# Moving four sums of a weight pair and a sum of squares from GpSimd's arithmetic to transfers and VectorE, and one PSUM copy to ScalarE

## The chip, the cores and the metric

The kernel runs on one core of a Trainium2 chip. Its time is the device time of one execution in microseconds. Names of the engines as the profile writes them: PE is TensorE (PEld its weight loads), DVE is VectorE, ACT is ScalarE, POOL is GpSimd, SP is the engine that issues most transfers. SPq, ACTq and POOLq are the queues from which transfers are issued.

## The reference, cut to what matters

One step of two trunk layers of a streaming encoder over 656 tokens (528 prompt rows with 16 learned ones, 128 sample rows), all in float32. Each layer is a feed-forward part, a mixer (pooling, short convolution, attention, gates, `w_out`), and a second feed-forward part:

```python
def swiglu(x, w_gate, w_up, w_down):
    return (jax.nn.silu(x @ w_gate) * (x @ w_up)) @ w_down

h = x + 0.5 * swiglu(rmsnorm(x, n1), f1g, f1u, f1d)      # 1024 -> 2816 -> 1024
...                                                       # mixer, added to h
h = h + 0.5 * swiglu(rmsnorm(h, n2), f2g, f2u, f2d)
```

The change touches only how the gate and up products (`x @ w_gate`, `x @ w_up`) get their weights, how one of their blocks leaves PSUM, and how the mean of squares of an rmsnorm is summed.

## The kernel before, in words

Activations stand transposed: 128 features in the partitions, tokens along the row. A float32 product is made of three passes over a high and a low part of weight and activation (`mm3`), so each weight block is split by a copy on ACT and a subtraction on DVE into a "slab" (`prep_next`, L338; the tile is called `ws` or `slabs`, 128x2x4x128).

Gate and up columns are worked in **pairs** of two 128-column blocks (`pair_unit`, L615). The pair is a 2x2 block matrix a11, a12, a21, a22 (`A1` holds a11 and a12, `A2` holds a21 and a22; both are raw weights as loaded, 512 KB each) and it is multiplied in seven block products instead of eight, in the manner of Strassen and Winograd. Besides raw blocks this wants four sums of weights (`sums`, L391): s3 = a11 + a21 (into a buffer of its own in the tile `Wa`, two of them in turn), a21 += a22, a11 += a21, a12 += a11, the last three in place. The seven slabs are, in order, a11, a12, the summed a21, the summed a11, the summed a12, s3 and the raw a22 (`prep_pair`, L385). There are 80 pairs: ten gate and ten up pairs in each of four feed-forward parts.

`run_pair` (L687) runs the seven products of 12 matmuls each (`seven`) into three PSUM banks. Bank b1 (tile `mm`) takes four of them one after the other: B11, Q2, T3 and T4. Between two of them the bank's content is copied out: after B11 and Q2 by ACT, after T3 by DVE as s[3] = b1 + p5 (L719). T4 adds to the same bank, so its first matmul waits until the reader after T3 is done. T4 is held back (`late`) until the first product of the next pair has been issued. T4's own result leaves by `stt`.

Loads go through four raw buffers in turn; a pair takes two and a down unit one. A buffer's next load waits for the last reader of the old content. Slabs have eight places; a slab's place comes free when its matmuls are done. Units follow each other as gate pair, eight down units of the chunk before, up pair, then gate and up pairs in turn.

After each `w_down` or `w_out` product of the last chunk `feed` (L508) adds the square of the new rows to a running sum `acc`: eight squares by ACT, of which the first starts the sum, numbers two to seven are added by POOL (L528), and the eighth by DVE. Then matmuls with a matrix of ones (`scales`) give the row scales for the next part. This happens five times; there are 30 POOL additions in all.

The order of instructions within each engine is set by a scheduler that reorders independent instructions; every engine, and every queue that issues transfers, then runs its instructions strictly in that order and each waits for what it needs.

Of the kernel before, what the change touches and what calls it, by code (L numbers as in the profile page):

```python
# [7 lines left out]
AF = mybir.ActivationFunctionType  # L8
ALU = mybir.AluOpType

P = 128
# [45 lines left out]
class Builder:  # L57
# [261 lines left out]
    def load_next(self):  # L319
        u = self.units[self.n_load]  # L320
        if self.n_done < u["after"]:
            return False
        spots = self.take("raw", len(u["src"]), u["ring"] == "F")
        if spots is None:
            return False
        u["raw"] = []
        for at, (k, parts) in zip(spots, u["src"]):
            raw = at
            if raw is None:
                raw = self.rp.tile([P, KD * P], F32, tag="raw", name=self.name("raw"))  # L330
            raw = raw.rearrange("p (k c) -> p k c", k=KD)[:, :k, :]
            for k0, kn, src in parts:
                self.nc.sync.dma_start(raw[:, k0:k0 + kn, :], src.rearrange("(k p) c -> p k c", p=P))
            u["raw"].append((at, raw))
        self.n_load += 1
        return True

# [47 lines left out]
    def prep_pair(self, u, i):  # L385
# [2 lines left out]
        s3 = self.s3[u["turn"]].rearrange("p (k c) -> p k c", k=4)  # L388
        return (A1[:, 0:4], A1[:, 4:8], A2[:, 0:4], A1[:, 0:4], A1[:, 4:8], s3, A2[:, 4:8])[i]

    def sums(self, u, i):  # L391
        if i == 1:
            (_, A1), (_, A2) = u["raw"]
            add = lambda out, a, b: self.nc.gpsimd.tensor_tensor(out, a, b, op=ALU.add)  # L394
            s3 = self.s3[u["turn"]].rearrange("p (k c) -> p k c", k=4)
            a11, a12, a21, a22 = A1[:, 0:4], A1[:, 4:8], A2[:, 0:4], A2[:, 4:8]
            add(s3, a11, a21)
            add(a21, a21, a22)
            add(a11, a21, a11)
            add(a12, a11, a12)  # L400


    def run_units(self, units):
# [104 lines left out]
    def feed(self, to, l, m, hi):  # L508

        c0, c1 = self.halves[hi]  # L510
        gain = {"mixer": "mix_norm", "ffn1": "ffn1_norm", "ffn2": "ffn2_norm"}[to]
        if to == "mixer":
            self.gained(self.H[:, m, c0:c1], l, m, c0, c1, gain)
        if hi == 0:
            return
        c0 = self.halves[0][0]
        n = c1 - c0
        if to != "mixer":
            self.blocks(l, m, gain, c0, n // 2)
        acc, s = self.acc[:, :n], self.sq[self.fed % 2][:, :n]  # L520
        if self.fed == 0:
            self.act(acc, self.H[:, m, c0:c1], AF.Square)
        else:
            self.act(s, self.H[:, m, c0:c1], AF.Square)
            if self.fed == KD - 1:
                self.tt(acc, acc, s, ALU.add)
            else:
                self.nc.gpsimd.tensor_tensor(acc, acc, s, op=ALU.add)  # L528
        self.fed += 1
        if self.fed == KD:  # L530
            self.fed = 0
            halves = self.halves
            self.pending = lambda: self.scales(to, halves)
# [81 lines left out]
    def pair_unit(self, w, f, run, **kw):  # L615

        c = [slice((f + r) * P, (f + r + 1) * P) for r in range(2)]
        self.turn = not self.turn
        return dict(slabs=[4] * 7, src=[(KD, [(0, KD, w[:, x])]) for x in c], prep=self.prep_pair, then=self.sums,
                    run=self.run_pair, evict=run, ring="F", turn=int(self.turn), **kw)  # L620

    def col_unit(self, w, f, r, run):

# [63 lines left out]
    def run_pair(self, u):  # L687

        c0 = self.halves[0][0]
        n = self.halves[0][1] - c0  # L690
        b1, b2, b3 = self.psum("mm"), self.psum("z"), self.psum("z")
        p5 = self.copies[u["turn"]][:, :n]
        f = self.factor[:, c0:c0 + 2 * n]
        S = self.sil if u["evict"] == self.gate_out else self.up
        S = S[:, :4 * n]
        s = [S[:, i * n:(i + 1) * n] for i in range(4)]
        self.clock += 1
        self.seven(u, b1, B11, n, True)
        self.act(s[0], b1[:, :n], AF.Copy)
        self.pump(1)  # L700
        if self.late:
            self.late()
        self.finish_pending()
        self.seven(u, b3, B21, n, True)
        self.tt(s[0], b3[:, :n], s[0], ALU.add)
        self.pump(1)
        self.seven(u, b2, Q1, n, True)
        self.act(p5, b2[:, :n], AF.Copy)
        self.pump(1)
        self.seven(u, b1, Q2, n, False)  # L710
        self.act(s[1], b1[:, :n], AF.Copy)
        self.pump(1)
        self.seven(u, b2, B22, n, False)
        self.tt(s[1], b2[:, :n], s[1], ALU.add)
        self.mul(S[:, :2 * n], S[:, :2 * n], f)
        u["evict"](u, 0, n)
        self.pump(1)
        self.seven(u, b1, T3, n, False)
        self.tt(s[3], b1[:, :n], p5, ALU.add)  # L719
        self.stt(s[3], s[3], -1.0, f[:, n:], ALU.mult, ALU.mult)  # L720
        self.pump(1)

        def last():
            self.late = None
            self.seven(u, b1, T4, n, False)
            self.stt(s[2], b1[:, :n], -1.0, f[:, :n], ALU.mult, ALU.mult)
            u["evict"](u, 1, n)
            self.pump(1)
        self.late = last
        self.slot_tail()  # L730
# [507 lines left out]
    def token_scale(self, hi, sums):  # L1238
        c0, c1 = HALF_ALL[hi]
        self.scale_of(sums, c0, c1, False, self.sil, self.up)  # L1240
# [343 lines left out]
```

## Time and profile before

| what | value |
| --- | --- |
| time, median of 3 | 2890.72 us (2889.88 to 2891.71) |
| the profiled execution | 2890.04 us, its span 2888.3 us |
| PE busy | 2829.0 us, 98% of the span |
| DVE, ACT, POOL busy | 1936.6, 1289.9, 598.2 us |
| granted TensorE clock, mean | 0.994 |
| DMA | 224.27 MB, mean 78 GB/s, busy share of the 16 engines 26.2% for the SP queue |

Busy PE time is nearly the whole span, so what can be read for a change is in the 59 us in which PE is not busy: which wait, at which place, and what released it. The rest of the engines matter as far as they end those waits.

### The profile page before, as it was taken

Reading aid. Unit: us, or ns where it says so; the run is one execution under the profiler, and the core shown is the slowest. Engines: PE = TensorE matmul, PEld = TensorE weight load, DVE = VectorE, ACT = ScalarE, POOL = GpSimd, SP = SyncE. Lnnn points to the kernel's source line nnn. Section 1 sums busy time; section 2 is a strip of 40 time slices with the busy share of each in tenths; the row PEclk is TensorE's granted clock in tenths of the full one; section 3 lists DMA queues with packets and bytes.
Section 4 is the critical chain, followed back from the end, with each engine's and each line's share of the span. In section 5 each row is a group of like instructions: output and inputs, shape, how many; then the busy total and the mean of one; then the engine's idle time right before and its main releaser. Section 6 shows DMA issues by size and latency. Waiting matters only on the chain.

```text
span 2888.3 us, 47733 instructions
## 1 busy us (share of the span) xinstructions
PE 2829.0 (98%) x19179; PEld 2781.5 (96%) x19179; DVE 1936.6 (67%) x3262; ACT 1289.9 (45%) x2464; POOL 598.2 (21%) x481
## 2 busy tenths in 40 slices
PE   7999999999999999999999999999999999999999
PEld 6999999999999999999999999999999999999999
DVE  8686675876444877675786675768764458675764
ACT  5343344776323443343443443447763234343433
POOL 2233231011000123132223241311110002232230
PEclk8999999999999999999999999999999999999999
DMA  3222322222222322222312322222222223223222
GB/s 113 81 86 69 88 76 74 79 77 69 66 74 74 88 81 66 82 80 74 88 52 81 88 74 81 83 71 72 75 73 66 79 75 88 76 67 92 81 71 76
DMA packets 437169, 224.27 MB, mean 78 GB/s; under 512 B 10110, under 2 KB 436290, under 8 KB 436946
## 3 DMA queue, kind: packets, MB, share of 16 engines
q1 hardware_dynamic: 436452, 220.90, 26.2%
q8 instruction: 150, 2.46, 0.3%
q14 instruction: 73, 0.60, 0.1%
q10 hardware_dynamic: 494, 0.32, 0.0%
HBM read 212.87 MB, written 8.31 MB: 77 GB/s over the span
## 4 chain that ended last, share of the span: by engine, by line
PE 81%; DVE 10%; POOL 4%; DMA 3%; ACT 1%; issue 1%; ACTq 0%; SPq 0%; POOLq 0%; DVEq 0%
PE z L143 50%; PE mm L143 29%; DVE Wa L134 2%; DMA rawb<-in_ffn_w_up_dram 2%; DVE ws L134 2%; DVE Wa L131 2%; DVE slabs L134 2%; POOL rawb L394 1%; POOL raw L394 1%; DVE XR L134 1%; POOL Wa L394 1%; DMA raw<-in_ffn_w_gate_dram 1%; PE aux L143 1%; ACT ws L120 0%; DVE ra L134 0%
## 5 line engine op out<-in xcount | busy, mean ns | idle before, releaser
L143 PE MATMUL mm<-XR,ws 128*128 128x328 f32 (+3 forms) x4848 | 802.6, 314 | 12.6 <-DVE Wa L134 12.6
L143 PEld LDWEIGHTS mm<-XR,ws 128*128 128x128 f32 x4848 | 738.0, 188 | 20.4 <-DVE Wa L134 16.0
L143 PE MATMUL z<-XR,ws 128*128 128x328 f32 (+3 forms) x3924 | 629.2, 313 | 13.5 <-ACT XR L120 6.5
L143 PEld LDWEIGHTS z<-XR,ws 128*128 128x128 f32 x3924 | 597.1, 189 | 15.3 <-ACT XR L120 6.8
L134 DVE TENSOR_TENSOR ws<-raw,ws 128x512 fp32r<-128x512 f32 (+1 forms) x429 | 311.2, 728 | 175.8 <-ACT ws L120 174.0
L143 PE MATMUL z<-ra,ws 128*128 128x328 f32 (+1 forms) x2688 | 421.0, 312 | 0.2
L120 ACT ACTIVATE ws<-raw 128x512 fp32r<-128x512 f32 (+1 forms) x429 | 263.5, 617 | 338.2 <-PE z L143 192.7
L143 PEld LDWEIGHTS z<-ra,ws 128*128 128x128 f32 x2688 | 405.1, 188 | 0.7 <-ACT ra L120 0.4
L143 PE MATMUL z<-ra,slabs 128*128 128x328 f32 (+1 forms) x2112 | 330.9, 312 | 1.8 <-ACT ra L120 1.8
L143 PE MATMUL mm<-XR,slabs 128*128 128x328 f32 (+1 forms) x1944 | 318.9, 312 | 7.9 <-DVE Wa L134 7.7
L143 PEld LDWEIGHTS z<-ra,slabs 128*128 128x128 f32 x2112 | 319.3, 188 | 2.9 <-ACT ra L120 2.4
L143 PEld LDWEIGHTS mm<-XR,slabs 128*128 128x128 f32 x1944 | 296.4, 188 | 10.6 <-DVE Wa L134 9.8
L143 PE MATMUL z<-XR,slabs 128*128 128x328 f32 (+1 forms) x1764 | 296.6, 316 | 9.7 <-DVE Wa L134 6.5
L143 PEld LDWEIGHTS z<-XR,slabs 128*128 128x128 f32 x1764 | 275.1, 192 | 11.2 <-DVE Wa L134 7.0
L131 DVE SCALAR_TENSOR_TENSOR H<-z,H 128x328 f32<-128x328 f32 (+1 forms) x288 | 140.9, 492 | 130.5 <-PE z L143 130.1
L134 DVE TENSOR_TENSOR Wa<-Wa 128x656 f32<-128x656 f32 (+5 forms) x245 | 204.3, 834 | 3.9 <-ACT Wa L120 0.2
L134 DVE TENSOR_TENSOR ws<-rawb,ws 128x512 fp32r<-128x512 f32 (+1 forms) x183 | 147.9, 812 | 83.2 <-ACT ws L120 82.9
L120 ACT ACTIVATE slabs<-raw 128x512 fp32r<-128x512 f32 (+1 forms) x183 | 109.0, 600 | 209.9 <-PE z L143 86.1
L120 ACT ACTIVATE Wa<-Wa 128x656 f32<-128x656 f32 (+7 forms) x232 | 136.9, 597 | 122.6 <-DVE Wa L134 113.6
L134 DVE TENSOR_TENSOR slabs<-raw,slabs 128x512 fp32r<-128x512 f32 (+1 forms) x183 | 145.9, 799 | 61.7 <-ACT slabs L120 61.5
L120 ACT ACTIVATE ws<-rawb 128x512 fp32r<-128x512 f32 (+1 forms) x183 | 108.3, 599 | 172.5 <-PE z L143 94.7
L528 POOL TENSOR_TENSOR Wa<-Wa 128x656 f32<-128x656 f32 (+1 forms) x30 | 55.1, 1837 | 628.7 <-ACT Wa L120 602.5
(177 smaller groups left out, 2943.4 us busy)
## 6 DMA issues: line engine op xcount, KB each, us to landing
raw<-in_w_in_dram SPq DMA_DIRECT2D x88, 512.0 KB, 3.8
raw<-in_ffn_w_gate_dram SPq DMA_DIRECT2D x57, 512.0 KB, 3.7
rawb<-in_ffn_w_up_dram SPq DMA_DIRECT2D x55, 512.0 KB, 4.3
rawb<-in_ffn_w_down_dram SPq DMA_DIRECT2D x48, 384.0 KB, 3.4
raw<-in_ffn_w_down_dram SPq DMA_DIRECT2D x48, 384.0 KB, 3.4
raw<-in_ffn_w_up_dram SPq DMA_DIRECT2D x33, 512.0 KB, 3.7
rawb<-in_ffn_w_gate_dram SPq DMA_DIRECT2D x31, 512.0 KB, 3.8
raw<-in_w_out_dram SPq DMA_DIRECT2D x16, 512.0 KB, 3.9
```

The costliest lines, as they stand in the source:

```text
L120: i = self.nc.scalar.activation(out, in_, func, **kw).ins
L131: return self.nc.vector.scalar_tensor_tensor(out, in0, scalar, in1, op0=op0, op1=op1).ins
L134: self.nc.vector.tensor_tensor(out, in0, in1, op=op)
L143: self.nc.tensor.matmul(out, lhsT, rhs, start=start, stop=stop, skip_group_check=True)
L394: add = lambda out, a, b: self.nc.gpsimd.tensor_tensor(out, a, b, op=ALU.add)
L528: self.nc.gpsimd.tensor_tensor(acc, acc, s, op=ALU.add)
```

## The change

Two of the four sums are made by transfers that add to what stands at their destination (`grow`, issued from POOL's queue with `accum_op`), as soon as the weights are loaded: a21 += a22, and s3, into which a21 is first loaded from DRAM once more (256 KB on SP's queue) and to which a11 is then added. The other two, a11 += a21 and a12 += a11, become DVE additions, issued when slab 2 has been prepared. POOL's additions of squares become adding transfers too. The copy of bank b1 after T3 goes to ACT, and DVE adds p5 afterwards, from SBUF to SBUF.

```diff
@@ load_next, after the raw loads of a unit @@
+        if "turn" in u:
+            self.early_sums(u)
@@
+    def early_sums(self, u):
+        (_, A1), (_, A2) = u["raw"]
+        s3 = self.s3[u["turn"]].rearrange("p (k c) -> p k c", k=4)
+        self.nc.sync.dma_start(s3, u["a21"])
+        self.grow(A2[:, 0:4], A2[:, 4:8])
+        self.grow(s3, A1[:, 0:4])
+
     def sums(self, u, i):
-        if i == 1:
+        if i == 2:
             (_, A1), (_, A2) = u["raw"]
-            add = lambda out, a, b: self.nc.gpsimd.tensor_tensor(out, a, b, op=ALU.add)
-            s3 = self.s3[u["turn"]].rearrange("p (k c) -> p k c", k=4)
-            a11, a12, a21, a22 = A1[:, 0:4], A1[:, 4:8], A2[:, 0:4], A2[:, 4:8]
-            add(s3, a11, a21)
-            add(a21, a21, a22)
-            add(a11, a21, a11)
-            add(a12, a11, a12)
+            self.tt(A1[:, 0:4], A2[:, 0:4], A1[:, 0:4], ALU.add)
+            self.tt(A1[:, 4:8], A1[:, 0:4], A1[:, 4:8], ALU.add)
+
+    def grow(self, to, by):
+        self.nc.gpsimd.dma_start(to, by, accum_op=ALU.add)
@@ feed @@
-                self.nc.gpsimd.tensor_tensor(acc, acc, s, op=ALU.add)
+                self.grow(acc, s)
@@ run_pair, after T3 @@
-        self.tt(s[3], b1[:, :n], p5, ALU.add)
+        self.act(s[3], b1[:, :n], AF.Copy)
+        self.tt(s[3], s[3], p5, ALU.add)
```

The scheduler gives other orders. First POOL, at the last gate pair of the first feed-forward part (its weights are raw_249 and raw_250, those of the up pairs beside it rawb, s3 a part of Wa). Before:

```order
L394 TENSOR_TENSOR Wa_86<-raw_249_3611,raw_250_3613 128x512
L394 TENSOR_TENSOR raw_250_3613<-raw_250_3613 128x512
L394 TENSOR_TENSOR rawb_3_105<-rawb_3_105 128x512 x2
L394 TENSOR_TENSOR Wa_86<-rawb_3_105 128x512
L394 TENSOR_TENSOR rawb_3_105<-rawb_3_105 128x512
L394 TENSOR_TENSOR raw_249_3611<-raw_250_3613,raw_249_3611 128x512
L394 TENSOR_TENSOR raw_249_3611<-raw_249_3611 128x512
```

The same pair with the one before and the one after it, of the change:

```order
L410 DMA Wa_86<-rawb_3_105 128x512
L410 DMA rawb_3_105<-rawb_3_105 128x512
L410 DMA Wa_86<-raw_249_3647 128x512
L410 DMA raw_250_3649<-raw_250_3649 128x512
L410 DMA Wa_86<-rawb_3_105 128x512
L410 DMA rawb_3_105<-rawb_3_105 128x512
```

Before, the third and fourth sum of the gate pair stand behind the first two sums of the up pair that is loaded after it; now each pair has two transfers, and nothing of a pair stands behind the next pair's.

Then the reader of bank b1 after T3 (mm_255), which T4 waits for: before on DVE, in the same pair's neighbour.

```order
L134 TENSOR_TENSOR Wa_86<-z_256_3720,Wa_86 128x328
L134 TENSOR_TENSOR Wa_86<-Wa_86 128x656
L134 TENSOR_TENSOR ws_259_3803<-raw_249_3611,ws_259_3803 128x512
L134 TENSOR_TENSOR Wa_86<-Wa_86 128x656
L134 TENSOR_TENSOR ws_260_3823<-raw_249_3611,ws_260_3823 128x512
L134 TENSOR_TENSOR ws_261_3840<-Wa_86,ws_261_3840 128x512
L134 TENSOR_TENSOR Wa_86<-mm_255_3719,Wa_86 128x328
```

Of the change it is on ACT, where the copy of the summed a21 (ws_258) and those of the other sums (ws_259, ws_260, ws_261) stand in the same queue:

```order
L120 ACTIVATE ws_254_3737<-rawb_3_105 128x512
L120 ACTIVATE ws_258_3824<-raw_250_3649 128x512
L120 ACTIVATE slabs_2_104<-Wa_86 128x512
L120 ACTIVATE Wa_86<-mm_246_3631 128x328
...
L120 ACTIVATE ws_259_3842<-raw_249_3647 128x512
L120 ACTIVATE ws_260_3862<-raw_249_3647 128x512
L120 ACTIVATE ws_261_3880<-Wa_86 128x512
...
L120 ACTIVATE ra_41_550<-Wa_86 128x656
L120 ACTIVATE Wa_86<-mm_255_3757 128x328
```

The reader of the bank has moved from a place behind three DVE subtractions of slabs to one behind their three copies on ACT, and the copy of the summed a21 stands ahead of the previous pair's s3 slab.

## Rows read from the trace of the kernel before

**Rows 1.** The page's part 1: busy time, share of the span, instructions.

```profile
PE 2829.0 (98%) x19179; PEld 2781.5 (96%) x19179; DVE 1936.6 (67%) x3262; ACT 1289.9 (45%) x2464; POOL 598.2 (21%) x481
```

**Rows 2.** Waits of PE over the span: total us, times, longest.

```profile
PE mm L143 <- DVE Wa L134: 20.3, 19, 1.8
PE z L143 <- DVE Wa L134: 10.1, 3, 3.9
PE z L143 <- DVE XR L134: 5.8, 2, 3.3
```

**Rows 3.** Timeline of PE in the second mixer: start, length, idle before.

```profile
1940.00 5.33 PE L143 MATMUL mm<-XR,ws 128*128 128x384 f32 x20 [1.77 <-DVE Wa L134]
```

**Rows 4.** Timeline of all engines, 406 to 418 us.

```profile
406.40 1.30 POOL L394 TENSOR_TENSOR Wa<-rawb 128x512 f32<-128x512 f32 x1 [8.53 <-DMA rawb<-in_ffn_w_up_dram]
...
409.51 1.28 POOL L394 TENSOR_TENSOR raw<-raw,raw 128x512 f32<-128x512 f32 x1
...
410.83 0.63 ACT L120 ACTIVATE ws<-raw 128x512 fp32r<-128x512 f32 x1 [5.76 <-POOL raw L394]
...
411.49 1.22 DVE L134 TENSOR_TENSOR ws<-raw,ws 128x512 fp32r<-128x512 f32 x1 [3.09 <-ACT ws L120]
...
414.59 0.49 DVE L134 TENSOR_TENSOR Wa<-mm,Wa 128x328 f32<-128x328 f32 x1
...
415.13 2.08 PE L143 MATMUL mm<-XR,slabs 128*128 128x328 f32 x12 [1.55 <-DVE Wa L134]
```

**Rows 5.** Who waited for line L394: total us, times.

```profile
  ACT slabs L120: 93.7, 42
  ACT ws L120: 70.6, 46
```

**Rows 6.** Timeline of PE at the layer boundary.

```profile
1462.51 5.58 PE L143 MATMUL z<-XR,slabs 128*128 128x328 f32 x25 [2.57 <-DVE XR L134]
...
1482.28 9.47 PE L143 MATMUL z<-XR,ws 128*128 128x328 f32 x51 [3.59 <-DVE Wa L134]
```

**Rows 7.** Windows: length, PE, PEld, DVE, ACT, POOL busy (instructions), clock, DMA, GB/s.

```profile
110.00:160.00 50.00, 50.00 (x336) 50.00 (x334) 34.01 (x50) 17.95 (x32) 17.35 (x12) 1.00 0.20 57
...
252.00:330.00 78.00, 76.12 (x506) 75.58 (x505) 61.10 (x88) 37.07 (x70) 27.76 (x18) 1.00 0.28 80
```

**Rows 8.** Groups by form, DVE, 745 to 940 us, where POOL is idle.

```profile
L134 DVE TENSOR_TENSOR ws<-raw,ws 128x512 fp32r<-128x512 f32 x54 | 37.3, 691 | 46.3 <-ACT ws L120 46.3
```

**Rows 9.** Groups by form, DVE, 252 to 330 us, six pairs with POOL's sums.

```profile
L134 DVE TENSOR_TENSOR ws<-raw,ws 128x512 fp32r<-128x512 f32 x8 | 7.5, 934 | 1.2 <-ACT ws L120 1.2
L134 DVE TENSOR_TENSOR slabs<-rawb,slabs 128x512 fp32r<-128x512 f32 x7 | 6.7, 962 | 0.3 <-ACT slabs L120 0.3
```

**Rows 10.** Groups by form over the span, ACT's copies of bank b1.

```profile
L120 ACT ACTIVATE Wa<-mm 128x328 f32<-128x328 f32 x120 | 51.9, 432 | 30.8 <-PE mm L143 30.2 <-DVE Wa L134 0.3
```

**Rows 11.** Timeline of all engines, 430 to 520 us, end of a sum of squares.

```profile
478.69 1.62 POOL L528 TENSOR_TENSOR Wa<-Wa 128x656 f32<-128x656 f32 x1 [4.20 <-ACT Wa L120]
...
483.22 0.74 ACT L120 ACTIVATE Wa<-H 128x656 f32<-128x656 f32 x1
...
484.06 0.84 DVE L134 TENSOR_TENSOR Wa<-Wa 128x656 f32<-128x656 f32 x1 [0.15 <-ACT Wa L120]
...
487.73 1.27 PE L143 MATMUL aux<-Wa,ones 128*128 128x328 f32 x4
```

**Rows 12.** DMA issues: count, KB each, median us from issue to landing.

```profile
raw<-in_ffn_w_gate_dram SPq DMA_DIRECT2D x57, 512.0 KB, 3.7
rawb<-in_ffn_w_down_dram SPq DMA_DIRECT2D x16, 256.0 KB, 2.8
```

**Rows 13.** The chain that ended last: start, length; its longest transfer.

```profile
2433.53 6.40 DMA rawb<-in_ffn_w_up_dram
```

**Rows 14.** Timeline of POOL, 160 to 460 us.

```profile
390.43 1.29 POOL L394 TENSOR_TENSOR Wa<-raw,raw 128x512 f32<-128x512 f32 x1 [9.31 <-DMA raw<-in_ffn_w_gate_dram]
...
394.21 3.67 POOL L394 TENSOR_TENSOR rawb<-rawb 128x512 f32<-128x512 f32 x2 [0.63 <-DVE slabs L134]
```

More of the change, by code (lines that the diff above doesn't have):

```diff
@@ L619, in pair_unit @@
         return dict(slabs=[4] * 7, src=[(KD, [(0, KD, w[:, x])]) for x in c], prep=self.prep_pair, then=self.sums,
-                    run=self.run_pair, evict=run, ring="F", turn=int(self.turn), **kw)
+                    run=self.run_pair, evict=run, ring="F", turn=int(self.turn),
+                    a21=w[0:4 * P, c[1]].rearrange("(k p) c -> p k c", p=P), **kw)
     def col_unit(self, w, f, r, run):
```

## The prediction, written before the changed kernel ran

> **What bounds the kernel now.** I read the busy times first: PE works 2829.0 of 2888.3 us [rows 1], so nothing that happens on another engine counts unless it takes from the 59 us in which PE stands. The list of PE's waits says how much of that this change can reach. 20.3 us in 19 waits are `mm` matmuls that wait for a DVE result in `Wa` [rows 2]; one of them, 1.77 us, lies in the second mixer [rows 3], so 18.5 us in 18 waits, about 1 us each, are T4 products of pairs that wait for s[3] = b1 + p5. Only 18 of 80 pairs wait at all. The other waits of size (`z` on `Wa`, `z` on `XR`) lie at the start and between stages.
>
> The timeline of one such wait tells its cause [rows 4]. POOL stands until 406.40 for the load of the *next* up pair, because that pair's first sum is ahead of the third sum of the gate pair in POOL's order. The third sum ends at 410.8; ACT, whose next row is the copy of that sum, has waited 5.76 us for it, DVE 3.09 us for ACT, and behind two more subtractions DVE reaches the s[3] addition at 414.59. PE then has lost 1.55 us. The reader is to see that the place where PE waits (DVE) is not what is late: POOL's order is. Over the whole run ACT waits 93.7 + 70.6 = 164 us in 88 waits for POOL's sums [rows 5]; some 18.5 us of it reaches PE.
>
> Two waits at the boundary between the layers, 2.57 and 3.59 us [rows 6], also lie where POOL's sums and squares run beside DVE. The rest of PE's idle time (the loads at the start, the other row scales, the end of the run) the change doesn't touch.
>
> **The change part by part.**
>
> *POOL's 320 sums go.* With them goes the blocking just read. If every T4 wait went, 18.5 us.
>
> *Two DVE additions per pair.* In a stretch of six pairs DVE is busy for 61.1 of 78 us [rows 7]. A 128x512 operation on it takes 0.691 us where POOL is idle [rows 8]; the 160 new ones are 110 us, 12 x 0.691 = 8.3 us in that stretch. There two groups of the same size take 934 and 962 ns while POOL reads [rows 9]; without POOL they would give back 8 x 0.243 + 7 x 0.271 = 3.8 us, and the other groups something besides. So DVE ends between 61 and 65.6 us of 78, 78 to 84%. What it delays is hidden as long as slabs are ahead of PE: a pair takes PE 84 x 0.149 = 12.5 us (336 matmuls in 50 us [rows 7]), and eight slabs, more than a pair's worth, can wait for PE. I take zero; if that cover were gone the additions would show in full, 110 us, and I see no reason for it at 84%.
>
> *The copy of b1 by ACT.* 80 copies of 0.43 us [rows 10], 35 us on an engine that is busy 45%. T4 now waits for an ACT row that stands behind the copies of the summed slabs, not behind their subtractions as well. Counted from the end of the product before T3, an up pair needs on DVE 0.49 + 0.69 + 0.84 + 0.69 + 0.84 = 3.6 us (s[1], two slabs, two products of 656 columns) and on ACT 0.74 + 0.43 for the high part of the activation and the bank, so the copy is there at 4.7 us [rows 4, 8, 10, 11]. PE has 23 matmuls to the end of T3 and by the new order 25 more to T4, 48 x 0.149 = 7.1 us. So 2.4 us are to spare, and the copy is hidden unless ACT is stopped ahead of it.
>
> *What can stop ACT now: the adding transfers.* The trace has no transfer within SBUF and none that adds. Nearest below is a plain 256 KB load, 2.8 us, and 512 KB take 3.7 [rows 12], so 0.9 us per 256 KB. An adding transfer reads source and destination and writes, three times 256 KB, which by that slope would be 2.8 + 1.8 = 4.6 us; nearest above is the longest load of the chain, 6.4 us [rows 13]. I take L = 4.6 and keep 2.8 and 6.4 for the range. The Trainium skill's page "DMA: Bandwidth & Descriptors" (Anatomy of one DMA) gives a fit for a transfer issued from GpSimd, 2.0 us plus bytes over 436 GB/s; the estimate from it for 256 KB is 2.6 us, near the lower end, and the sum would be 2870 by it. No run here shows it yet.
>
> When must it have landed? The gate pair of [rows 4] had its weights at 390.43 [rows 14]. s3's load now stands between the two raw loads on SP's queue and takes its share, so A2 lands 0.9 us later, at 391.3; plus 4.6 is 395.9. In the new order ACT's copy of the summed a21 comes right after the copies of the previous pair's third and fourth sums, which before could not be made until POOL's sums of 394.21 to 397.9 had ended [rows 14]. With those sums on DVE that point comes one to two microseconds earlier, so 395.9 is about on time: at some pairs ACT waits a microsecond or two, at most none. Before, 164 us of ACT's waits became 18.5 us of PE's; for 40 waits of 1.5 us the same ratio gives 7 us, and I take 6 as new waits. At L = 2.8 it is none, at 6.4 about what was there before.
>
> *Squares.* 30 POOL additions become transfers of 336 KB. By the slope L is 3.1 us for the bytes once, 4.3 for twice and 5.4 for three times; I take 4.9, and the ends are 3.1 and 6.4. A square follows the next in 5.4 us (36 matmuls x 0.149; additions 478.69 and 484.06 [rows 11]), or 7.1 us after `w_out` (48 matmuls). As long as L stays under 5.4 the last, DVE's, waits for nothing. I take zero; see the first rival.
>
> *Layer boundary.* Of the 6.2 us [rows 6] I take 2 as gone, with DVE no longer slowed by POOL's reads; bounds 0 and 6.2.
>
> *Transfers for s3 and the rest.* 20 MB more loads and the adding transfers meet 16 engines that are busy 28% in the pair stretch [rows 7]; hidden.
>
> **The sum.** -18.5 + 6 - 2 = -14.5 us against the profiled execution's 2890.04 us, 2875.5. The median of the three runs is 0.7 us above the profiled one, so the forecast is 2876 us. Its own range: -18.5 - 6.2 gives 2866, and half of the gain spent on new waits 2884.
>
> **The rivals.**
>
> *Squares in a queue (slower).* If an adding transfer of 336 KB takes more than 5.4 us, each waits for the one before, and after six of them DVE's final addition is 6 x (L - 5.4) late. DVE stands in order, so evictions and slabs behind it stand too. PE has 2.8 us to spare (addition ends 484.9, the ones matmul starts 487.73 [rows 11]). At L = 8: three sums at the quick pace, 3 x (15.6 - 2.8) = 38 us, two after `w_out`, 2 x (5.4 - 2.8) = 5 us, 43 in all; less the gain, 2890.7 + 43 - 14.5 = 2919 us. It outweighs the gain from L of about 6.6 (3 x 4.4 + 0 = 13 us) on. For it: no row bounds what adding costs, and POOL issues in order. Against: the longest plain transfer in the chain is 6.4 us, and three times the bytes, 5.4, still keeps the pace. The Trainium skill speaks against this use: the page "SBUF — State Buffer" (Summary: rules for kernel authors) advises against hiding a GpSimd-issued DMA under DVE, whose two-port modes keep its descriptors from being written. Another section (Who interferes with whom) excepts `tensor_tensor`, which is what most DVE rows of these stretches are; were it to hold all the same, one DVE operation of 0.7 us would bring L to 5.6 at my value, and the sum would stay, since 6 x 0.2 is within the 2.8 us; at three times the bytes it would be 3 x (4.2 - 2.8) = 4 us more, 2880.
>
> *The gain is turned into waits for transfers (no change).* With L near 6.4, a summed a21 lands at 397.7, which is when POOL's sums ended before (397.9), and ACT stands ahead of the bank copy as it stood before. PE's waits keep their number and change their name from DVE to ACT: 2888 us. For it: the scheduler put that copy early, and ACT is the engine whose lateness decides now. Against: the third sum no longer waits for another pair's load, the worst of the waits (5.76 us). It is also how the change would fail to do what it says: a T4 that waits as long for ACT as for DVE.
>
> *All of it (faster yet).* L under 4 us and the boundary freed: 2866 us.
>
> **How the numbers follow.** Within 0.2%, or 5.8 us, a measurement of this kernel can't be told from no change, so faster means under 2885. Forecast 0.60, all of it 0.09, turned into waits 0.14 (0.11 within 0.2%, 0.03 faster), squares in a queue 0.15 (0.13 slower, 0.02 within), a full DVE or something unread 0.02 (slower). Faster 0.72, same 0.13, slower 0.15. The range 2866 to 2898 leaves out a tenth above, where L is over 6.9 us, and some below.
>
> **What would show it.** POOL busy falls from 598 to some 50 us. The DVE groups of 128x512 in a stretch of pairs come down to near 0.7 us. PE's `mm` waits for DVE go to a few us, and new ones for ACT are under 8 us. ACT's waits for POOL become waits for transfers of a pair, under 80 us in all. The final addition of squares starts right after its square. It is wrong if PE waits over 10 us for ACT in pairs, if DVE stands for a transfer ahead of the row scales, or if L, from issue to release, is above 5.4 us.

## The result and the profile after

The changed kernel takes 2852.2 us (median of 4 runs, 2851.5 to 2854.4) beside 2890.3 us of the kernel before: ratio 0.9871, 95% interval 0.9854 to 0.9889. That is 38 us faster, and below the predicted range of 2866 to 2898; the forecast was 14.5 us. The profiled execution took 2852.4 us, its span 2850.7.

The page's part 1, after [rows 1]:

```profile
PE 2821.5 (99%) x19179; PEld 2781.3 (98%) x19179; DVE 1853.5 (65%) x3422; ACT 1320.7 (46%) x2544; POOL 222.5 (8%) x321
```

The span is 37.6 us shorter, and 7.5 us of this is *busy* PE time, with the same 19179 matmuls. So idle time was not the whole price of a wait. Those of PE's waits that matter here, after [rows 2], total us, times, longest:

```profile
PE z L143 <- DVE Wa L134: 7.3, 2, 4.1
PE z L143 <- ACT XR L120: 6.6, 2, 5.5
PE mm L143 <- DVE Wa L134: 2.1, 2, 1.8
PE z L143 <- DVE H L131: 1.4, 1, 1.4
```

Of the 18 T4 waits none is left, and ACT took none over: 1.8 of the 2.1 us is the wait in the second mixer [rows 3]. The view's lines for the weight loads of PE tell these waits nearly with their full price, first of before, then of after:

```profile
PEld mm L143 <- DVE Wa L134: 25.9, 22, 2.0
```

```profile
PEld mm L143 <- DVE Wa L134: 2.8, 3, 2.0
```

The same gate pair as in [rows 4], PE in the changed kernel; the row at 408.14 is T4:

```profile
406.33 1.97 PE L143 MATMUL z<-XR,ws 128*128 128x328 f32 x12
408.14 1.98 PE L143 MATMUL mm<-XR,slabs 128*128 128x328 f32 x12
```

and ACT's copy of the bank ahead of it with the DVE addition behind the copy:

```profile
405.13 0.43 ACT L120 ACTIVATE Wa<-mm 128x328 f32<-128x328 f32 x1
```

```profile
406.01 0.49 DVE L134 TENSOR_TENSOR Wa<-Wa 128x328 f32<-128x328 f32 x1
```

ACT's copy ends at 405.56, so the bank is free 2.6 us before T4 starts; the prediction had 2.4 us to spare.

To see where the 38 us come from I cut both traces at the same matmuls: PE's order of stages is the same, so the start of matmul number k can be set beside the start of number k. Start to start, in us (pairs are the stages ffn1 and ffn2 of both layers, without the start and the boundary; row scales are the stretches after both `w_out` and around the second mixer's start):

| kernel | start | pairs | boundary | row scales | mixers | median us |
| --- | --- | --- | --- | --- | --- | --- |
| before | 82.7 | 1572.4 | 70.5 | 239.8 | 916.8 | 2890.3 |
| changed | 79.3 | 1545.5 | 60.7 | 242.7 | 916.8 | 2852.2 |

Pairs give 26.9 us, the layer boundary 9.8, the start 3.4, and the row scales take 2.9 back: 37.2 in sum.

In the boundary the two waits of [rows 6], 6.2 us, are gone, and with them 3.6 us behind them, mostly slow matmuls. Windows behind both waits, of before (length, PE, PEld, DVE, ACT, POOL busy, granted clock, DMA, GB/s):

```profile
1462.50:1468.10 5.60, 5.59 (x27) 5.59 (x28) 5.60 (x7) 3.12 (x4) 1.09 (x1) 0.70 0.21 61
1482.30:1490.00 7.70, 7.70 (x41) 7.70 (x42) 5.76 (x12) 3.75 (x5) 0.00 (x0) 0.78 0.00 0
```

The same matmuls as in the first, after:

```profile
1446.00:1451.60 5.60, 5.60 (x39) 5.58 (x38) 4.84 (x8) 0.93 (x2) 0.89 (x1) 1.00 0.68 139
```

27 matmuls in 5.6 us at a granted clock of 0.70, against 39 at 1.00: behind each of these stands of 2.6 and 3.6 us (PE waited for DVE) part of the matmuls ran at the lower of the two levels, 1.2 GHz. PE counts as busy there, so this price stands in no list of waits. In the pairs the stands are shorter and the clock stays at 1.00; what comes on top of a T4 wait there is about 0.27 us each time (0.21 to 0.34 at 14 of the 18). For the wait of 1.55 us in [rows 4] the next matmuls have fallen 1.82 us further behind the same ones after.

DVE in the window of six pairs [rows 7, 9], after, and two of its groups:

```profile
252.00:330.00 78.00, 78.00 (x521) 78.00 (x521) 59.64 (x100) 39.98 (x77) 5.99 (x7) 1.00 0.49 124
```

```profile
L134 DVE TENSOR_TENSOR ws<-raw,ws 128x512 fp32r<-128x512 f32 x8 | 5.5, 689 | 2.3 <-ACT ws L120 2.2
L134 DVE TENSOR_TENSOR slabs<-rawb,slabs 128x512 fp32r<-128x512 f32 x7 | 4.7, 682 | 0.0
```

934 and 962 ns became 689 and 682, and twelve more additions in DVE's order cost nothing in sum: 61.1 us busy before, 59.6 after.

The adding transfers (KB each, median us from issue to landing):

```profile
raw<-raw POOLq DMA_DIRECT2D x40, 256.0 KB, 3.2
Wa<-raw POOLq DMA_DIRECT2D x40, 256.0 KB, 4.1
Wa<-Wa POOLq DMA_DIRECT2D x24, 328.0 KB, 4.1
Wa<-Wa POOLq DMA_DIRECT2D x6, 320.0 KB, 4.9
```

Who waited for them over the run (us, times):

```profile
  ACT slabs L120: 19.9, 11
  DVE rawb L134: 15.3, 3
  POOL Wa L410: 12.5, 3
  DVE raw L134: 7.2, 3
  ACT ws L120: 1.7, 3
```

ACT's 164 us of [rows 5] are 21.6. But DVE stands for a transfer in six places, 22.5 us, and this reaches PE at the row scales and in the first down stage. The longest PE wait is at the row scales after the first `w_out`. POOL, DVE and PE there:

```profile
1004.09 0.87 POOL L410 DMA_DIRECT2D Wa<-rawb  x1 [1.93 <-DMA rawb<-in_ffn_w_gate_dram]
```

```profile
1011.80 0.69 DVE L134 TENSOR_TENSOR rawb<-raw,rawb 128x512 f32<-128x512 f32 x1 [5.21 <-DMA Wa<-rawb]
1012.41 0.49 DVE L131 SCALAR_TENSOR_TENSOR Wa<-Wa 128x328 f32<-128x328 f32 x1
```

```profile
1017.23 9.38 PE L143 MATMUL z<-XR,slabs 128*128 128x328 f32 x51 [4.13 <-DVE Wa L134]
```

DVE's a11 += a21 overwrites what the transfer s3 += a11 still reads. That transfer, issued among raw loads, took 7.5 us; the row scales' own operations stand behind the addition. Only this stand and one of 3.9 us after the second `w_out`, 9.1 us in both, are for the reading of a11. In the other four, 13.4 us, the same addition stands for the summed a21 itself, the result of the other transfer. The longest of them is in the first down stage, where PE then waits 1.4 us (`z` on `H` above):

```profile
111.08 0.69 DVE L134 TENSOR_TENSOR rawb<-rawb 128x512 f32<-128x512 f32 x1 [6.26 <-DMA rawb<-rawb]
```

### The profile page after: what moved, and what is told of

Its sections match the earlier page's. It is cut to its first block, busy times and chain, and to the rows that moved or that the text cites. A ratio compares the mean times of both kernels' runs of the same rounds, so it can differ in the third digit from the quotient of the medians.

```text
span 2850.7 us, 48269 instructions
## 1 busy us (share of the span) xinstructions
PE 2821.5 (99%) x19179; PEld 2781.3 (98%) x19179; DVE 1853.5 (65%) x3422; ACT 1320.7 (46%) x2544; POOL 222.5 (8%) x321
## 4 chain that ended last, share of the span: by engine, by line
PE 96%; DMA 2%; DVE 1%; ACT 1%; issue 0%; POOL 0%; ACTq 0%; SPq 0%; DVEq 0%; POOLq 0%
PE z L143 59%; PE mm L143 36%; PE aux L143 1%; DMA Wa<-rawb 0%; DMA raw<-in_ffn_w_gate_dram 0%; DVE Wa L131 0%; DMA raw<-in_ffn_w_up_dram 0%; DVE XR L134 0%; PE aux L1088 0%; DMA rawb<-in_ffn_w_gate_dram 0%; DMA rawb<-rawb 0%; ACT Wa L120 0%; DVE ws L134 0%; PE aux L1068 0%; DMA Wa<-in_k_norm_dram 0%
## 5 line engine op out<-in xcount | busy, mean ns | idle before, releaser
L134 DVE TENSOR_TENSOR ws<-raw,ws 128x512 fp32r<-128x512 f32 (+1 forms) x429 | 287.9, 673 | 176.7 <-ACT ws L120 175.3
L134 DVE TENSOR_TENSOR Wa<-Wa 128x328 f32<-128x328 f32 (+5 forms) x325 | 215.2, 668 | 36.4 <-ACT Wa L120 33.0
L120 ACT ACTIVATE Wa<-mm 128x328 f32<-128x328 f32 (+1 forms) x240 | 105.5, 439 | 148.9 <-PE mm L143 147.9
L120 ACT ACTIVATE slabs<-rawb 128x512 fp32r<-128x512 f32 (+1 forms) x181 | 107.6, 599 | 143.8 <-PE z L143 99.3
L134 DVE TENSOR_TENSOR ws<-rawb,ws 128x512 fp32r<-128x512 f32 (+1 forms) x183 | 118.8, 652 | 61.0 <-ACT ws L120 60.1
```

The costliest lines, as they stand in the source:

```text
L120: i = self.nc.scalar.activation(out, in_, func, **kw).ins
L134: self.nc.vector.tensor_tensor(out, in0, in1, op=op)
```

## The experiments

Two theories. **A**, of the prediction: POOL's order is late (a pair's third sum behind the next pair's first), and ACT with it. **B**: DVE's order is late, since the bank's reader stands behind three subtractions. A rival to both, **C**: DVE is slow because POOL reads beside it. The first four kernels are the change in pieces; all stage sums stand in one table at the end.

**Only the bank copy (e1).**

```diff
@@ kernel before, run_pair @@
-        self.tt(s[3], b1[:, :n], p5, ALU.add)
+        self.act(s[3], b1[:, :n], AF.Copy)
+        self.tt(s[3], s[3], p5, ALU.add)
```

> The kernel before with one edit: the copy of bank b1 after T3 goes to ScalarE, VectorE adds p5 from SBUF. Theory A (GpSimd's order is late, as predicted): ACT still stands for the sums, so PE's T4 waits stay, now named ACT, and the time is within 5 us of 2890. Theory B (VectorE's place behind three subtractions is late): the T4 waits go, 18 of them with about 1.3 us each, and the time falls by 20 us or more, to 2870 or below.

Measured: 2876.7 us, ratio 0.9952 (0.9937 to 0.9967); pairs 1556.3. It lies between the two forecasts: 14 us. ACT waits for POOL's sums as long as before (us, times; [rows 5]), and PE's `mm` waits for ACT are few:

```profile
  ACT slabs L120: 97.3, 52
  ACT ws L120: 68.8, 49
```

```profile
PE mm L143 <- ACT Wa L120: 5.4, 8, 1.4
```

So A in its strong form, that POOL's lateness passes to PE whoever reads the bank, falls: for most of it the DVE part of the chain (a subtraction for each late copy) is a necessary link too. With the copy alone the pairs gain 16 of the 27 us.

**Only the sums (e2)**: the changed kernel with `self.tt(s[3], b1[:, :n], p5, ALU.add)` and POOL's `tensor_tensor(acc, acc, s)` put back.

> The changed kernel with two edits undone (bank b1 read by VectorE, squares added by GpSimd), so only the four sums differ from before. Theory A: nearly all of the gain in the pairs (28.8 us of the two traces) is there, 2858 to 2865 by whether the layer boundary comes with it. Theory B: T4 still waits for VectorE in some 15 places, 2875 to 2885.

Measured: 2855.7 us, 0.9879 (0.9862 to 0.9895); pairs 1547.4, boundary 64.6. As A expected, even a little under its range: no T4 wait in the pairs, with the reader on DVE. Beside the sums the copy is worth some 2 us in the pairs (1545.3 in e4 below).

**Only the squares (e3)**: the kernel before with

```diff
@@ feed @@
-                self.nc.gpsimd.tensor_tensor(acc, acc, s, op=ALU.add)
+                self.nc.gpsimd.dma_start(acc, s, accum_op=ALU.add)
```

> The kernel before with the 30 additions of squares as adding transfers, nothing else. If the squares' GpSimd arithmetic caused the two waits at the layer boundary (9.8 us in the traces, their aftermath included), 2880; if the pairs' sums caused them, within 3 us of 2890, the boundary's two waits still there.

Measured: 2885.7 us, 0.9984 (0.9974 to 0.9993). Between the two cases: the boundary falls to 65.5 from 70.5, and one of its two waits, 3.0 us, is left. **The change with POOL's squares (e4)** is the same edit undone in the changed kernel.

> The changed kernel with the 30 additions of squares back on GpSimd's arithmetic. If the squares made the boundary's gain, 2862 with its waits of 2.6 and 3.6 us back; if the sums made it, 2850 to 2854, and the wait of 4.1 us after w_out of the first layer, which follows a VectorE addition that stood for a pair's transfer, is unchanged.

Measured: 2856.6 us, 0.9878 (0.9862 to 0.9893), boundary 63.8, pairs 1545.3. Neither case held whole: sums alone bring the boundary from 70.5 to 64.6, squares alone to 65.5, both to 60.7. Each part takes one of the two waits of [rows 6]: with the squares still on POOL (e2, e4) the first is left, 2.1 and 2.6 us, and with the sums still on POOL (e3) the second, 3.0 us. There C is at work. Just ahead of the first wait, in the kernel before, POOL adds a square beside the DVE operation for which PE waits:

```profile
1459.93 1.82 POOL L528 TENSOR_TENSOR Wa<-Wa 128x656 f32<-128x656 f32 x1
1460.25 2.20 DVE L134 TENSOR_TENSOR XR<-Wa,XR 128x656 fp32r<-128x656 f32 x1
```

In the changed kernel the same DVE operation takes 0.83 us. One group of row-scale operations of DVE at the boundary, of before, of the sums alone, and of the changed kernel:

```profile
L131 DVE SCALAR_TENSOR_TENSOR Wa<-Wa 128x328 f32<-128x328 f32 x8 | 8.1, 1013 | 0.1
```

```profile
L131 DVE SCALAR_TENSOR_TENSOR Wa<-Wa 128x328 f32<-128x328 f32 x8 | 7.0, 869 | 0.0
```

```profile
L131 DVE SCALAR_TENSOR_TENSOR Wa<-Wa 128x328 f32<-128x328 f32 x8 | 3.9, 491 | 0.0
```

Before, these take twice their time on average where POOL's additions run, on an engine that is busy without a gap (5.60 of 5.60 us in the first window above), with PE waiting behind.

**Order or contention in the pairs.** Two kernels keep POOL reading beside DVE but give the third and fourth sum to DVE. In the first (e5) the changed kernel's two early sums are POOL arithmetic:

```diff
@@ changed kernel, early_sums @@
-        self.nc.sync.dma_start(s3, u["a21"])
-        self.grow(A2[:, 0:4], A2[:, 4:8])
-        self.grow(s3, A1[:, 0:4])
+        add(s3, A1[:, 0:4], A2[:, 0:4])           # gpsimd.tensor_tensor
+        add(A2[:, 0:4], A2[:, 0:4], A2[:, 4:8])
```

> The changed kernel, but the two early sums (a21 += a22 and s3) by GpSimd's arithmetic in place of adding transfers; the other two stay on VectorE, squares as transfers, bank copy by ScalarE. Nothing of a pair stands behind the next pair's sums, but GpSimd's reads slow VectorE again in half of the places. If the order was the harm, 2850 to 2857. If the slowed VectorE was, half of what the sums gave beside the copy is lost, 2863 or more.

The second (e11) is the kernel before with one edit, and the bank still read by DVE:

```diff
@@ kernel before, sums: the last two moved to i == 2 @@
-            add(a11, a21, a11)
-            add(a12, a11, a12)
+        if i == 2:
+            (_, A1), (_, A2) = u["raw"]
+            self.tt(A1[:, 0:4], A2[:, 0:4], A1[:, 0:4], ALU.add)
+            self.tt(A1[:, 4:8], A1[:, 0:4], A1[:, 4:8], ALU.add)
```

> The kernel before with one edit: the third and fourth sum of a pair by VectorE, issued after slab 2; the first two stay GpSimd arithmetic, bank b1 is read by VectorE, squares by GpSimd. GpSimd still reads beside VectorE, but no sum stands behind the next pair's. If the order alone makes the pairs' waits, the four pair stages come from 1572 to about 1550 us and the time to 2862 to 2868; if the slowed VectorE or the place of the bank's reader is needed too, 2875 or more.

Measured: e5 2860.3 us, 0.9892 (0.9877 to 0.9906), pairs 1543.9; e11 2862.8 us, 0.9904 (0.9888 to 0.9921), pairs 1547.0. The pairs are as quick as in the changed kernel. e5's whole time lies between the two forecasts, but what it lacks isn't in the pairs. DVE in the six-pair window of e5, and a group there:

```profile
252.00:330.00 78.00, 78.00 (x522) 78.00 (x521) 67.17 (x101) 39.97 (x77) 12.76 (x8) 1.00 0.29 84
```

```profile
L134 DVE TENSOR_TENSOR ws<-raw,ws 128x512 fp32r<-128x512 f32 x8 | 7.5, 942 | 0.2
```

DVE is as slow as before (942 ns) and busier than ever, 86%, and PE doesn't stand once. In e11 those who waited for POOL's two sums, over the run:

```profile
  DVE raw L134: 3.4, 2
  ACT slabs L120: 1.0, 2
  DVE rawb L134: 0.8, 1
```

One edit took ACT's 164 us to 1.0, so the place of these two sums makes the waits, as A has it, and C is rejected for the pairs. The trace of before agrees: of its 18 T4 waits 15 lead back, over the copy that ACT made late, to a POOL sum that stood behind the next pair's first two sums, and in 12 of these POOL had stood 7.8 to 9.7 us for the next pair's load. What no run separates is that the two sums are also quicker on DVE (0.82 to 0.93 us in e11, 1.3 us and more on POOL); no kernel kept them on POOL in a better order.

**No transfers at all (e6)**: the kernel before with all four `add` as `self.tt` on DVE.

> The kernel before with all four sums by VectorE, no transfer, no GpSimd in the pairs; bank b1 still read by VectorE, squares by GpSimd. 24 additions of 0.69 us more in six pairs bring VectorE to about 66 of 78 us. If GpSimd (its order or its reads) was the harm, the time comes to 2855 to 2865 without any transfer. If VectorE's queue decides (T4 behind subtractions, now also behind additions), T4 waits stay and it is 2880 or more.

Measured: 2858.6 us, 0.9888 (0.9873 to 0.9902); pairs 1549.5. The first case; 62.7 of 78 us of DVE in the window. So adding transfers aren't needed for the gain.

**What the transfers cost (e7, e8).** In e7 s3's second block is added straight from DRAM, so DVE's addition no longer waits for s3's transfer:

```diff
-        self.grow(s3, A1[:, 0:4])
+        for h in (0, 2):
+            self.grow(s3[:, h:h + 2], u["a11"][:, h:h + 2])   # a11 of the DRAM weight
```

> The changed kernel, but s3's second block is added straight from DRAM (two transfers of 128 KB for each pair), so that VectorE's a11 += a21 no longer waits until the transfer has read a11. If those waits (5.2 us at the row scales after w_out, 6.3 us at 111 us) are the price of the change, PE's waits of 4.1 and 1.4 us behind them shrink: 2846 to 2850. If the transfers from DRAM in small pieces are slower or GpSimd's third issue is late, new waits for s3: 2853 to 2862.

Measured: 2868.0 us, 0.9922 (0.9906 to 0.9939). Both parts of the expectation happened. Row scales went from 242.7 to 234.3, and no DVE stand for s3's transfer is left, so the price read above was real; the wait at 111 us, which the expectation counts with it, was for a21. But pairs rose to 1561.6, with 13 waits of bank products for ACT, which stands 44.9 us for the later landing of a21 (21.6 in the changed kernel):

```profile
PE mm L143 <- ACT Wa L120: 11.1, 13, 1.6
```

The mixers rose by 6.6 us, most of it at one PE wait of 3.5 us in the second mixer, whose cause is open.

In e8 the other two sums are transfers as well, where DVE's additions stood (`self.grow(A1[:, 0:4], A2[:, 0:4])` and `self.grow(A1[:, 4:8], A1[:, 0:4])`).

> The changed kernel with the other two sums as adding transfers too, issued where VectorE's additions stood. They form a chain, each of 3.2 us and more, and stand in GpSimd's order near the next pair's transfers. If ScalarE has that slack, VectorE is 110 us freer and the time is 2850 to 2853. If not, ScalarE waits for a11 and a12 in the pairs and PE behind it: 2870 to 2900.

Measured: 2940.7 us, 1.0175 (1.0159 to 1.0190), slower and beyond the range given. The pairs take 1642.5. Who waited for the transfers, and PE's waits for ACT:

```profile
  ACT slabs L120: 220.7, 78
  ACT ws L120: 196.6, 79
  POOL rawb L410: 100.3, 36
  POOL raw L410: 99.6, 34
```

```profile
PE mm L143 <- ACT Wa L120: 63.6, 46, 3.5
```

A chain of transfers late in a pair has the trouble of POOL's old order over again: each waits for the landing of the one before, and what stands behind it in POOL's order waits too (100.3 and 99.6 us).

**Towards a better kernel.** e9 is e6 with the bank copy and the squares as transfers, e10 is e6 with the bank copy only.

> The kernel before with all four sums on VectorE (no GpSimd, no transfers, no second load of a21), the bank copy on ScalarE and the squares as adding transfers. If the price of the adding transfers in the changed kernel is VectorE's wait for them around the row scales, its pair stages keep the changed kernel's 1545 us and the three stages of row scales and the boundary come down by about 8 us: 2842 to 2847, faster than the changed kernel's 2852. If VectorE with 220 us of additions is too full behind a copy, 2855 or more.

> As the kernel beside it (four sums on VectorE, bank copy on ScalarE), but the squares added by GpSimd as before. If GpSimd's reads beside a full VectorE keep a wait at the layer boundary alive, some 3 us more than with transfers, 2845 to 2850; if the transfers of squares are what is late at the row scales, the same or less.

Measured: e9 2854.2 us, 0.9870 (0.9856 to 0.9885); e10 2852.0 us, 0.9867 (0.9851 to 0.9883). e9 missed: the pairs and the boundary came as expected, but the row scales stayed at 239.8 and the start at 84.2; e10 has 233.5 and 82.7, and is level with e9, its second case, though the boundary kept the 3 us of its first. In both the four sums stand in DVE's order among the row scales and wait there for loads; what makes 6 us between them is not settled. Both are level with the changed kernel.

e12 puts together the best of each stage, e13 is the changed kernel again:

```diff
@@ e12, over e10, abridged @@
+        first=self.pairs <= 2      # these two pairs: early_sums and DVE as in the change
+        if to == "ffn1": self.grow(acc, s)   # else gpsimd.tensor_tensor
```

> Pieces put together by the stages of the earlier runs: four sums on VectorE and the bank copy on ScalarE (pairs at 1544 us), but the first two pairs with the change's adding transfers (start 3 us shorter than with VectorE's sums, which stand there for loads), squares as transfers only at the layer boundary (2.9 us less than with GpSimd there) and by GpSimd elsewhere (row scales after w_out 4 and 3 us shorter than in the changed kernel). If the stages add, 2852.0 - 3.2 - 2.9 = 2846. If the stages don't add, no better than the changed kernel: 2850 to 2854.

> The changed kernel as it is, beside the mixed one: 2852, as measured before. The profile of a second execution tells whether the wait of 4.1 us after the first w_out and the one of 1.4 us in the first down stage are of this kernel (both again, within 1 us) or of one execution.

Measured: e12 2847.0 us, 0.9855 (0.9840 to 0.9869); e13 2852.7 us, 0.9879 (0.9863 to 0.9896). The time is the one expected if the stages add, though the start was no shorter (83.9, with 3.8 us of waits for the input). e12 has the lowest median of all, but its interval overlaps by a little with that of e13 and more with those of e9 and e10. In e13 the addition after `w_out` stands again, but shorter, and PE's wait fell from 4.13 to 2.61, before's level:

```profile
1009.54 0.69 DVE L134 TENSOR_TENSOR rawb<-raw,rawb 128x512 f32<-128x512 f32 x1 [3.51 <-DMA Wa<-rawb]
```

```profile
1014.98 7.25 PE L143 MATMUL z<-XR,slabs 128*128 128x328 f32 x38 [2.61 <-DVE Wa L134]
```

and the wait of 1.4 us at 112 is 0.2. So DVE's stand is of the kernel; 1.5 and 1.2 us of what PE lost behind the two were that execution's.

| kernel | start | pairs | boundary | row scales | mixers | median us |
| --- | --- | --- | --- | --- | --- | --- |
| e1 copy | 87.6 | 1556.3 | 70.0 | 240.6 | 916.8 | 2876.7 |
| e2 sums | 82.3 | 1547.4 | 64.6 | 240.1 | 916.8 | 2855.7 |
| e3 squares | 83.8 | 1569.9 | 65.5 | 242.0 | 916.8 | 2885.7 |
| e4 change, POOL squares | 83.3 | 1545.3 | 63.8 | 240.0 | 916.8 | 2856.6 |
| e5 POOL early | 84.2 | 1543.9 | 62.0 | 245.5 | 916.8 | 2860.3 |
| e6 DVE sums | 83.4 | 1549.5 | 64.2 | 232.6 | 916.8 | 2858.6 |
| e7 from DRAM | 80.1 | 1561.6 | 60.7 | 234.3 | 923.4 | 2868.0 |
| e8 four transfers | 79.1 | 1642.5 | 60.6 | 232.4 | 916.8 | 2940.7 |
| e9 DVE, copy, squares | 84.2 | 1544.1 | 60.6 | 239.8 | 916.8 | 2854.2 |
| e10 DVE, copy | 82.7 | 1544.2 | 63.5 | 233.5 | 916.8 | 2852.0 |
| e11 two on DVE | 83.0 | 1547.0 | 66.5 | 238.4 | 916.8 | 2862.8 |
| e12 mixed | 83.9 | 1544.1 | 60.6 | 234.6 | 916.8 | 2847.0 |
| e13 change again | 79.8 | 1544.3 | 60.7 | 241.0 | 916.8 | 2852.7 |

Stages are of one execution each, the profiled one, which can lie some us off the median (e6 some 4 below it). The changed kernel and its repetition e13 differ by 1.2 us in the pairs and 1.7 at the row scales, so less than that tells nothing. The start holds waits for the input's load that differ from one execution to the next (0.6 us in the changed kernel, 3.8 in e12), so it tells less than the rest.

## Why the prediction was wrong

The sign and the cause of the T4 waits were right; the size was not, 38 us for 14.5. The step that failed is the price of a wait: the prediction counted only "the 59 us in which PE stands" and left out what the next matmuls lose, and 7.5 us of the gain is busy PE time. That made the pairs 8.4 us too small and, with the low guess of what would go, the boundary 7.8; a third term, 6 us of new waits for ACT, did not come. By its steps:

- **"If every T4 wait went, 18.5 us."** The waits went, for the reason given (e11). The term was too small: the pairs gave 26.9 us. I summed idle time of PE, and every T4 wait costs 0.27 us more. One of the 18 lies in the start; the 17 others are 18.1 us idle and 17 x 0.27 = 4.6 us, 22.7 in all, and the weight loads' rows above held that. Of the other 5.9 us (1.7 us of the new wait at 112 come off again) most are short waits in the same stages that I left as they were and that went too, before (total us, times, longest):

```profile
PE z L143 <- ACT ra L120: 1.8, 2, 0.9
PE z L143 <- DVE slabs L134: 0.6, 2, 0.3
```

- **"So 2.4 us are to spare, and the copy is hidden."** Right, 2.6 us at the pair shown, and no PE wait for ACT in any pair. That the copy alone would bring 14 us (e1) was not in it: I named POOL's order as what is late, and it needed DVE's three subtractions as well to reach PE.
- **"I take L = 4.6" and "+6 as new waits".** L was 3.2 to 4.1 us in the median. ACT waited for transfers 14 times, 21.6 us, not 40 times 1.5 us, and PE had no wait for ACT in the pairs. This term, 6 us of a 14.5 us sum, should have been zero for ACT. What I did not cost was DVE's a11 += a21, which needs the summed a21 and must also wait until the transfer into s3 has read a11. It stood 22.5 us in six places, four times for the one (13.4 us), twice for the other (9.1 us). PE lost 1.7 us by it in the first down stage, and 2.9 us more than before at the row scales (1.2 in the second execution, e13). I had only listed it among the signs of being wrong ("if DVE stands for a transfer ahead of the row scales"), and that sign came, as did L above 5.4 us, at 29 of 190 transfers. POOL's busy time fell to 222.5 us and not to some 50, as each issue of an adding transfer counts as 0.86 us of POOL.
- **"Of the 6.2 us I take 2 as gone."** The term furthest off for its size: 9.8. Both waits went whole, 6.2 us, and the 3.6 us behind them as well, mostly slow matmuls, which no list of waits holds. The upper bound I gave, 6.2, was itself too low for that reason. The cause I gave, DVE slowed by POOL, was right (1013 ns to 491); the 2 was a guess, and neither the sums nor the squares alone remove both waits (e2, e3).
- **Two DVE additions, zero.** Right as to their time: DVE is busy 59.6 of 78 us, and PE doesn't stand in that window.
- **Squares, zero.** Right as to the rival: the last addition starts 0.03 us after its square, and L was over 5.4 us in six of 30, five of them after `w_out`, where the pace is 7.1 us. POOL stood 12.5 us in three places for its own last transfer, without harm. Their gain at the boundary was missed.
- **The start**, which I said the change doesn't touch: 3.4 us in one execution, 2.9 in another, some 2.7 without the waits for the input. Two PE waits there (`z` on `XR`) are 9.8 us before and 6.4 after.

Sum by what was measured: -26.9 - 9.8 - 3.4 + 2.9 = -37.2 us, where I had -18.5 + 6 - 2.

The last square's rows after [rows 11], ACT, DVE and PE:

```profile
474.71 0.74 ACT L120 ACTIVATE Wa<-H 128x656 f32<-128x656 f32 x1
```

```profile
475.48 0.84 DVE L134 TENSOR_TENSOR Wa<-Wa 128x656 f32<-128x656 f32 x1
```

```profile
479.22 1.27 PE L143 MATMUL aux<-Wa,ones 128*128 128x328 f32 x4
```

The rivals: no queue of squares formed for which PE waited; the gain did not turn into waits; "all of it", 2866, was nearest and still 14 us high, as it counted idle time only.

## What to carry to other kernels

Price a wait of the bounding engine by what the next instructions lose, not by its idle time: take the same instructions of an unstalled place, or the weight loads' rows, and behind longer stands read the granted clock. When a helper engine's results come late, look at its order: moving the last two of four sums to another engine did nearly all that mattered in the pairs, and kernels with and without transfers, with a fast or a slowed VectorE, came out within 6 us of each other there. An accumulating transfer has two ends to wait for: whoever needs its result, and whoever overwrites its source (13.4 and 9.1 us of DVE's stands here).

## What the runs showed of the hardware

An adding transfer of 256 KB within SBUF took 3.2 us at the least. The longer ones go with other traffic: of the 190 in the changed kernel (30 of them squares, 320 or 328 KB), the 97 during whose first 3 us the rest of the transfers kept the 16 engines under 10% busy took 3.26 us in the median, the 67 at 30 to 60% took 4.7, and the three above 90% took 5.8, 7.4 and 7.7. No run varies the traffic alone. The fit of the Trainium skill, "DMA: Bandwidth & Descriptors" (Anatomy of one DMA), gave 2.6 us and is low by 0.6. The Trainium skill, "SBUF — State Buffer" (Summary: rules for kernel authors), advises against hiding a GpSimd transfer under VectorE, because of VectorE's 2x and 4x modes. With this kernel's VectorE operations, nearly all `tensor_tensor` and `scalar_tensor_tensor`, no cost shows: the 41 whose first 2.5 us VectorE filled to over 98% took 3.8 us in the median, the 11 with under 0.5 us of VectorE 4.9.

GpSimd's additions double the mean time of a group of VectorE's `scalar_tensor_tensor` at the boundary (491 to 1013 ns) and lengthen the 128x512 subtractions in the pairs by a third (689 to 934), both seen by taking the additions away.
